# Moving a kernel's stationary blocks by 4 to 124 bytes and its second slot of moving tiles by 32 bytes

## The chip, the cores and the metric

The kernel runs on one core of one Trainium2 chip. The metric is the device time in microseconds of one execution of the whole program; lower is better. The changed kernel computes the same outputs from the same inputs with one launch.

## What is computed

One inference step of a one-layer decoder trunk, for a prompt of 2048 tokens and a group of 64 sample tokens (2112 columns in all), D = 1024 channels, everything in float32:

```python
xn = _rmsnorm(h, norm_mix)
proj = xn @ w_in + b_in                      # 1024 x 9216
q, fz, iv, za, ga, gb, zb, ma, mb = jnp.split(proj, SPLIT_POINTS, axis=-1)
...                                          # recurrence over q, f, v gives o
y_a = (o * jax.nn.silu(za)) @ w_br_a         # 1024 x 1024
u = ga * jax.nn.sigmoid(gb)
...                                          # 31 taps of a depthwise convolution over u give cv
y_b = (cv * jax.nn.silu(zb)) @ w_br_b        # 1024 x 1024
merged = jax.nn.sigmoid(ma) * y_a + jax.nn.sigmoid(mb) * y_b
h = h + merged @ w_o
gate = jax.nn.sigmoid(_rmsnorm(h, norm_ple) @ w_ple_gate)
h = h + gate * (p_l @ w_ple)
```

Nearly all of the work is in the products with w_in, w_br_a and w_br_b (stage 1 and 2 of the kernel) and in those with w_o, w_ple_gate and w_ple (stage 3).

## The kernel before

A float32 product is made of three products in the type fp32r: each operand is split into a high part (a copy rounded to fp32r) and a low part (the rest), and hi*hi, hi*lo and lo*hi are summed in PSUM.

**Weights.** The three big weights are cut into 176 blocks of 128 output columns: 72 of w_in for each half of the tokens, then 16 blocks each of w_br_a and w_br_b. A block is loaded whole into a tile `raw` (128 partitions x 1024 numbers) and split by two instructions in `split_w`: ScalarE (ACT) writes `whi`, VectorE (DVE) writes `wlo`. The pool `wp` turns over three buffers of each; it lies at the right end of SBUF.

```python
    wp = st12.enter_context(tc.tile_pool(name="wp", bufs=3, side="right"))             # L113
    def split_w(b):                                                                    # L323
        b.hi = wp.tile([P, KB, P], F32R, tag="whi", name="whi")
        b.lo = wp.tile([P, KB, P], F32R, tag="wlo", name="wlo")
        nc.scalar.activation(out=b.hi, in_=b.raw, func=AF.Copy)                        # L326
        nc.vector.tensor_tensor(out=b.lo, in0=b.raw, in1=f32(b.hi), op=ALU.subtract)   # L327
```

**Moving tiles.** The activations stand in two slots, X[0] (`x0h`, `x0l`, 512 columns for each of 8 blocks of 128 channels) and X[1] (`x1h`, `x1l`, up to 576 columns), which `x_alloc` (L135) takes from the pool `xres` near the left end of SBUF; they are taken again from the same place for each new half of the tokens and for each stage.

**Units.** A unit is one block of weights times one stretch of 512, 320 or 256 columns of one slot: 24 matmuls (L1357), in which the weights are the stationary operand, loaded anew for every matmul by a LDWEIGHTS, and the slot is the moving one.

```python
        for k in range(KB):                                                            # L1353
            for w, x in ((u.block.hi, xh), (u.block.hi, xl), (u.block.lo, xh)):
                nc.tensor.matmul(ps[:, 0:u.n], lhsT=w[:, k, :], rhs=x[:, k, sl], ...)  # L1357
```

There are 441 units, so 10,584 such matmuls. Between and after them stand small matmuls and transposes of the recurrence (L441 to L594), the convolution's taps on DVE (L686 to L699), and the evacuations of PSUM. The program is ordered by hand: `at_time` gives each piece of side work a unit after which it is issued, and nothing of the order depends on addresses.

**Stage 3** (from L1371) computes the last three products for 17 blocks of tokens with one function `gemm` (L1182, matmuls at L1188). Here the tokens are the stationary operand (`mgi`, `th`, `tl`, `ph`, `pl`) and the weights the moving one (`woh`, `wol`, the slots X[0] and X[1] again, filled with w_ple_gate, and `wph`, `wpl`). Its pools take the room of stage 2 as that is freed. What it loads first is, in the order of SyncE's (SP's) queue: the last store of `mg` to the scratch tensor `mg_dr` (L908), the second `mgi` (L1166, `load_m`), the first `h` (L1175, `load`), then `p`, the second `h`, four loads for w_ple and eight for w_ple_gate (L1382), the norm vector (L1420), and the third `mgi`. The first `h` is needed by the first evacuation of `out_proj` (L1204) and, through a norm on ACT, POOL and DVE (L1281, L1287 to L1289, L1212), by the first transposes of `turn` (L1239).

**Where the tiles lie.** Addresses follow from the sizes of the tiles and the order in which they are taken; a partition holds what is counted here in bytes. In the program as built, all tiles that feed the matmuls of L1357 and L1188 start 96 bytes past a multiple of 128: `x0h` (at 18144), `x0l`, `x1h` (at 50912), `x1l`, the three buffers each of `whi` and `wlo` (from 204768), and in stage 3 `woh`, `wol`, `mgi`, `th`, `tl`, `ph`, `pl`, `wph`, `wpl`. Their slices for k and for columns start at multiples of 128 bytes from there. Among the tiles of the side work, `v`, `st`, `kt` and `kq` start 96 bytes past a multiple of 128 too, `at`, `s_all` and the inputs `xt` 32 bytes past, and `ident` at a multiple of it. `u`, the input of the convolution, starts 96 past a multiple of 128, and tap i reads it from 4*i bytes further on.

Of the kernel before, what the change touches and what calls it, by code (L numbers as in the profile page):

```python
# [9 lines left out]
F32 = mybir.dt.float32  # L10
F32R = mybir.dt.float32r
# [6 lines left out]
P = 128  # L18
KB = 8
# [55 lines left out]
def view(t, off, dims):  # L75
    return bass.AP(t.tensor, t.offset + off, [list(t.ap[0])] + [list(d) for d in dims])


def f32(ap):
    return ap.bitcast(F32)  # L80
# [3 lines left out]
def tile_hybrid_step(  # L84
# [7 lines left out]
    nc = tc.nc  # L92
# [16 lines left out]
    xres = ctx.enter_context(tc.tile_pool(name="xres", bufs=1))  # L109
# [3 lines left out]
    wp = st12.enter_context(tc.tile_pool(name="wp", bufs=3, side="right"))  # L113
# [21 lines left out]
    def x_alloc(slot, cap=None):  # L135
        cap = cap or (512, 576)[slot]
        X[slot] = (xres.tile([P, KB, cap], F32R, tag=f"x{slot}h", name=f"x{slot}h"),
                   xres.tile([P, KB, cap], F32R, tag=f"x{slot}l", name=f"x{slot}l"))
# [74 lines left out]
    x_load(3)  # L213
    every = ("tr", "ab", "kv", "o")
    x_alloc(0)
    x_alloc(1)

    vrow = h1.tile([P, P], F32, tag="sg", name="vrow")
# [102 lines left out]
        nc.sync.dma_start(out=b.raw, in_=b.src.rearrange("(k p) c -> p k c", p=P))  # L321

    def split_w(b):  # L323
        b.hi = wp.tile([P, KB, P], F32R, tag="whi", name="whi")
        b.lo = wp.tile([P, KB, P], F32R, tag="wlo", name="wlo")
        nc.scalar.activation(out=b.hi, in_=b.raw, func=AF.Copy)  # L326
        nc.vector.tensor_tensor(out=b.lo, in0=b.raw, in1=f32(b.hi), op=ALU.subtract)  # L327
        b.raw = None
# [725 lines left out]
    for e in range(2):  # L1054
        x_turn(0, e, every)
    split_w(blocks[0])
    load_raw(blocks[2])
    x_load(6)
# [8 lines left out]
    for i in range(9):  # L1067
        t, b = XOUT0 + XOUT_STEP * i, 8 + i
# [262 lines left out]
    for b in range(1, len(blocks)):  # L1331
        i = 1 if b == 2 else max(uses[b][0] - 3, 0)
        if b >= 3:
            i = max(i, min(uses[b - 3][-1] + 1, uses[b][0] - 1))
        slots.setdefault(i, []).append((1, 0.0, b, lambda b=b: split_w(blocks[b])))
        if b + 2 < len(blocks):
            slots.setdefault(i + RAW_LAG, []).append((4, 0.5, b, lambda b=b: load_raw(blocks[b + 2])))
# [128 lines left out]
```

## Time and profile before

| | us |
|---|---|
| two runs | 2846.43 and 2839.39, median 2842.91 |
| the profiled execution, its own time | 2839.55 |
| span of its profile, first to last instruction | 2837.8 |
| TensorE matmuls (PE) busy | 2791.2 |
| VectorE (DVE) busy | 1886.4 |
| ScalarE (ACT) busy | 930.6 |
| GpSimd (POOL) busy | 544.9 |

The profiled execution takes 1.75 us more than its span, before the first and after the last instruction. A matmul's recorded duration holds its way through the pipeline, so consecutive ones overlap; what one costs in a stream is the distance from its start to the start of the next, which the timeline shows. The two runs lie 7 us apart.

### The profile page before, as it was taken

How to read it: one execution, taken by the hardware profiler on the slowest of the kernel's cores; microseconds unless marked ns; L12 is line 12 of the kernel's file. 1: busy time of each engine (PE TensorE's matmuls, PEld its weight loads, DVE VectorE, ACT ScalarE, POOL GpSimd, SP SyncE). 2: the span in 40 equal slices, each digit the busy share in tenths (PEclk: the TensorE clock that was granted, in tenths of full speed). 3: DMA queues.
4: the chain of work that ended last, by engine and by line, in shares of the span. 5: the costliest groups of instructions: out<-in, count | busy, mean ns of one | idle time of the engine just before them, and what ended most of it. 6: DMA issues, size and time to landing. Idle time of an engine off the chain costs nothing. (4 is left out here: it accounts for less than half of the span.)

```text
span 2837.8 us, 50952 instructions
## 1 busy us (share of the span) xinstructions
PE 2791.2 (98%) x21199; PEld 2383.1 (84%) x21199; DVE 1886.4 (66%) x2994; ACT 930.6 (33%) x2119; POOL 544.9 (19%) x929
## 2 busy tenths in 40 slices
PE   8999999999999999999999999999999999999998
PEld 6888888888888898988888888888789789788887
DVE  6577777777878786666757576677777876433433
ACT  5333333333332432332322322233244443322222
POOL 2000000000000014233240505050536420000000
PEclk9999999999999999999999999999999999999999
DMA  3222222222221422222222222223586879422221
GB/s 122 65 66 82 72 86 90 83 82 64 81 64 59 131 65 74 65 71 66 79 62 65 73 66 69 59 83 103 164 272 208 260 253 299 149 80 78 87 88 39
DMA packets 352799, 292.69 MB, mean 103 GB/s; under 512 B 17514, under 2 KB 301259, under 8 KB 352568
## 3 DMA queue, kind: packets, MB, share of 16 engines
q1 hardware_dynamic: 293856, 218.40, 25.4%
q10 hardware_dynamic: 58440, 70.86, 7.4%
q8 instruction: 166, 2.72, 0.4%
q14 instruction: 65, 0.53, 0.1%
q0 software_dynamic: 272, 0.19, 0.0%
HBM read 201.25 MB, written 88.14 MB: 102 GB/s over the span
## 5 line engine op out<-in xcount | busy, mean ns | idle before, releaser
L696 DVE SCALAR_TENSOR_TENSOR acc<-u,cw,acc 128x512 f32<-128x512 f32 x960 | 726.2, 756 | 24.0
L1357 PE MATMUL mm<-x1h,whi 128*128 128x320 f32 (+2 forms) x2112 | 711.9, 337 | 0.0
L1357 PE MATMUL mm<-x1h,wlo 128*128 128x320 f32 (+2 forms) x2112 | 693.2, 328 | 0.0
L1357 PE MATMUL mm<-x1l,whi 128*128 128x320 f32 (+2 forms) x2112 | 692.7, 328 | 0.0
L1357 PE MATMUL mm<-x0h,whi 128*128 128x512 f32 (+1 forms) x1416 | 564.9, 399 | 1.5 <-ACT x0h L1031 1.1
L1357 PE MATMUL mm<-x0l,whi 128*128 128x512 f32 (+1 forms) x1416 | 551.9, 390 | 2.1 <-DVE x0l L176 1.8
L1357 PE MATMUL mm<-x0h,wlo 128*128 128x512 f32 (+1 forms) x1416 | 551.9, 390 | 0.0
L1357 PEld LDWEIGHTS mm<-x1h,whi 128*128 128x128 f32 x2112 | 401.3, 190 | 33.7 <-issue 4.7
L1357 PEld LDWEIGHTS mm<-x1h,wlo 128*128 128x128 f32 x2112 | 400.6, 190 | 28.7
L1357 PEld LDWEIGHTS mm<-x1l,whi 128*128 128x128 f32 x2112 | 401.5, 190 | 26.4
L327 DVE TENSOR_TENSOR wlo<-raw,whi 128x1024 fp32r<-128x1024 f32 x176 | 218.3, 1241 | 259.6 <-ACT whi L326 253.0
L1357 PEld LDWEIGHTS mm<-x0h,whi 128*128 128x128 f32 x1416 | 266.8, 188 | 59.3 <-ACT sp L780 2.6
L1357 PEld LDWEIGHTS mm<-x0h,wlo 128*128 128x128 f32 x1416 | 266.8, 188 | 56.8 <-DVE wlo L327 0.4
L1357 PEld LDWEIGHTS mm<-x0l,whi 128*128 128x128 f32 x1416 | 267.1, 189 | 53.8 <-DVE x0l L176 2.5
L326 ACT ACTIVATE whi<-raw 128x1024 fp32r<-128x1024 f32 x176 | 186.0, 1057 | 65.7 <-DVE mal L889 23.4
L560 POOL TENSOR_SCALAR ors<-oss 128x4 f32<-128x4 f32 (+1 forms) x40 | 11.6, 289 | 875.5 <-ACT on L558 874.7
L1188 PE MATMUL ps<-woh,mgi 128*128 128x512 f32 x528 | 169.4, 395 | 2.1 <-DMA mgi<-mg_dr 2.1
L419 DVE TENSOR_TENSOR rp<-rp 128x512 f32<-128x512 f32 (+1 forms) x224 | 156.8, 700 | 9.6
L429 DVE TENSOR_TENSOR lvl<-kq,rp 128x512 f32<-128x512 f32 (+2 forms) x224 | 146.8, 655 | 21.2 <-PE d32p L455 19.4
L747 POOL TENSOR_SCALAR nmix<-us,cw 128x64 f32<-128x64 f32 x240 | 156.6, 653 | 0.0
L1188 PEld LDWEIGHTS ps<-woh,mgi 128*128 128x128 f32 x528 | 99.9, 189 | 23.1 <-DMA mgi<-mg_dr 2.4
L780 ACT ACTIVATE sp<-mm,vcol 128x512 f32<-128x512 f32 (+2 forms) x120 | 73.1, 609 | 127.9 <-PE mm L1357 113.0
(254 smaller groups left out, 3345.9 us busy)
## 6 DMA issues: line engine op xcount, KB each, us to landing
raw<-in_w_in_dram SPq DMA_DIRECT2D x144, 512.0 KB, 3.9
mgi<-mg_dr SPq DMA_DIRECT2D x16, 1024.0 KB, 6.0
gate<-am_dr SPq DMA_DIRECT2D x24, 512.0 KB, 5.6
mg_dr<-mg SPq DMA_DIRECT2D x24, 512.0 KB, 3.4
xt<-in_x_prompt_dram SPq DMA_DIRECT2D x16, 512.0 KB, 5.1
g_dr<-gst ACTq DMA_DIRECT2D x32, 256.0 KB, 2.8
cv_dr<-acc ACTq DMA_DIRECT2D x32, 256.0 KB, 2.1
raw<-in_w_br_a_dram SPq DMA_DIRECT2D x16, 512.0 KB, 5.9
```

Of the source, the lines that this page charges most:

```text
L326: nc.scalar.activation(out=b.hi, in_=b.raw, func=AF.Copy)
L327: nc.vector.tensor_tensor(out=b.lo, in0=b.raw, in1=f32(b.hi), op=ALU.subtract)
L419: nc.vector.tensor_tensor(out=io, in0=io, in1=tt, op=ALU.mult)
L429: nc.vector.tensor_tensor(out=o, in0=a, in1=b, op=ALU.mult)
L560: nc.gpsimd.tensor_scalar(out=rs[0:n, 0:m], in0=ss[0:n, 0:m], scalar1=1.0 / P, scalar2=EPS, op0=ALU.mult, op1=ALU.add)
L696: nc.vector.scalar_tensor_tensor(out=self.acc, in0=self.u[:, i:i + G], scalar=w, in1=self.acc, op0=ALU.mult, op1=ALU.add)
L747: nc.gpsimd.tensor_scalar(out=p, in0=self.us[:, :, i:i + 8], scalar1=w, scalar2=None, op0=ALU.mult)
L780: nc.scalar.activation(out=s[:, 0:n], in_=ps[:, 0:n], func=func, bias=bias(kind, j))
L1188: nc.tensor.matmul(ps, lhsT=a[:, k, :], rhs=c[:, k, s], start=(k == 0 and i == 0), stop=(k == kn - 1 and i == len(ops) - 1))
L1357: nc.tensor.matmul(ps[:, 0:u.n], lhsT=w[:, k, :], rhs=x[:, k, sl], start=(k == 0 and w is u.block.hi and x is xh), stop=(k == KB - 1 and w ...
```

## The change

A gap of 8 numbers (32 bytes) is taken between X[0] and X[1], and cleared once by DVE, so that X[1] and all that is taken after it at the left lies 32 bytes further on. The buffers of `whi` and `wlo` become 32 numbers longer, and block i is written to, and read from, an offset of (i mod 32) numbers in its buffer; that is 4*(i mod 32) bytes, so that 32 blocks in turn go through all multiples of 4 from 0 to 124 bytes. So that all of this fits, the room that is kept for descriptors of POOL's DMAs is given as 8192 bytes a partition in place of 16384. The diff:

```diff
     x_alloc(0)
+    gap = xres.tile([P, 8], F32, name="gap")
+    nc.vector.memset(gap, 0.0)
     x_alloc(1)
...
     def split_w(b):
-        b.hi = wp.tile([P, KB, P], F32R, tag="whi", name="whi")
-        b.lo = wp.tile([P, KB, P], F32R, tag="wlo", name="wlo")
+        o = b.i % 32
+        b.hi = view(wp.tile([P, KB * P + 32], F32R, tag="whi", name="whi"), o, [[P, KB], [1, P]])
+        b.lo = view(wp.tile([P, KB * P + 32], F32R, tag="wlo", name="wlo"), o, [[P, KB], [1, P]])
...
-    nc = _bacc.Bacc("TRN2", target_bir_lowering=False, num_devices=1)
+    nc = _bacc.Bacc("TRN2", target_bir_lowering=False, num_devices=1, dynamic_dma_scratch_size=8192)
```

In the program as built, `x0h` and `x0l` still start 96 bytes past a multiple of 128. `x1h` and `x1l` start at a multiple of 128, and so do `woh`, `wol`, `mgi`, `th`, `tl`, `ph`, `pl`, `wph` and `wpl` of stage 3, and `v`, `st`, `kt`, `kq` and `u` of the side work. The weight buffers start 96 past a multiple of 128, 4224 bytes apart, and a block 4*(i mod 32) bytes after that.

No instruction changes its place on any engine. DVE has one more, at its start:

```order
L129 MEMSET mhalf 128x1
L131 MEMSET lead 128x16
L217 MEMSET gap 128x8
L295 MEMSET d32p 128x480
L298 MEMSET lvl_145 128x1152
```

The row of `gap` is new; the others stand as before, with line numbers two higher after it.

The tiles of stage 3 take over other bytes than before, and so some of them wait for something else. This is SP's queue where stage 2 ends, with the semaphores waited for; the eight names DMAHW0 to DMAHW7 are used by SP's DMAs in turn, and DMAHW3 at these rows is the one that the last store of `mg` (the first row) raises when it has landed. Before:

```order
L908 DMA mg_dr<-mg 128x2x320 [waits DMAHW3_49,DVE_49]
L1166 DMA mgi<-mg_dr 128x16x128 [waits DMAHW6_49,DMAHW4_49]
L1175 DMA h<-in_x_prompt_dram 128x1024 [waits DMAHW5_49,DMAHW0_49]
L1180 DMA p<-in_p_prompt_dram 128x256
L1175 DMA h<-in_x_prompt_dram 128x1024 [waits DMAHW7_49]
```

And now:

```order
L911 DMA mg_dr<-mg 128x2x320 [waits DMAHW3_49,DVE_49]
L1169 DMA mgi<-mg_dr 128x16x128 [waits DMAHW4_49,PE_49]
L1178 DMA h<-in_x_prompt_dram 128x1024 [waits DMAHW5_49,DMAHW7_49,DMAHW3_49,DMAHW1_49]
L1183 DMA p<-in_p_prompt_dram 128x256 [waits DMAHW6_49]
L1178 DMA h<-in_x_prompt_dram 128x1024 [waits DMAHW0_49]
```

The first `h` (third row) lies on bytes of an `mg` buffer now, and its load waits until the store in the first row has landed; before, it waited for earlier transfers only. PE's wait in the second row is for a transpose of the recurrence, far back.

## Rows read from the trace of the kernel before

**Rows 1.** The page: busy time by engine, TensorE's granted clock by slice, POOL's DMA queue.

```profile
PE 2791.2 (98%) x21199; PEld 2383.1 (84%) x21199; DVE 1886.4 (66%) x2994; ACT 930.6 (33%) x2119; POOL 544.9 (19%) x929
...
PEclk9999999999999999999999999999999999999999
...
q0 software_dynamic: 272, 0.19, 0.0%
```

**Rows 2.** Groups by line and shape on PE; moving operand first, then stationary.

```profile
line engine op names shapes xcount | busy us, mean ns | idle before us <-releasers
L1357 PE MATMUL mm<-x0h,whi 128*128 128x512 f32 x1400 | 559.0, 399 | 1.1 <-ACT x0h L1031 1.1
...
L1357 PE MATMUL mm<-x1h,whi 128*128 128x512 f32 x704 | 282.6, 401 | 0.0
...
L1357 PE MATMUL mm<-x1h,whi 128*128 128x320 f32 x704 | 223.6, 318 | 0.0
...
L1357 PE MATMUL mm<-x1h,whi 128*128 128x256 f32 x704 | 205.7, 292 | 0.0
...
L1188 PE MATMUL ps<-woh,mgi 128*128 128x512 f32 x528 | 169.4, 395 | 2.1 <-DMA mgi<-mg_dr 2.1
```

**Rows 3.** Timeline of PE, 2376 to 2388 us: 512, then 256 columns (start us, us).

```profile
2375.69 0.39 PE L1357 MATMUL mm<-x0h,wlo 128*128 128x512 f32 x1
...
2384.53 0.39 PE L1357 MATMUL mm<-x0h,wlo 128*128 128x512 f32 x1
...
2384.99 0.28 PE L1357 MATMUL mm<-x1h,wlo 128*128 128x256 f32 x1
...
2387.63 0.31 PE L1357 MATMUL mm<-x1h,whi 128*128 128x320 f32 x1
```

**Rows 4.** Timeline of PE, 1500 to 1502 us: 320 columns.

```profile
1499.80 0.31 PE L1357 MATMUL mm<-x1h,wlo 128*128 128x320 f32 x1
...
1502.00 0.31 PE L1357 MATMUL mm<-x1h,wlo 128*128 128x320 f32 x1
```

**Rows 5.** Timeline of PE after small matmuls of the recurrence, 789 to 792 us.

```profile
789.80 0.40 PE L1357 MATMUL mm<-x0l,whi 128*128 128x512 f32 x1
...
791.89 0.39 PE L1357 MATMUL mm<-x0l,whi 128*128 128x512 f32 x1
```

**Rows 6.** Groups on PEld: the weight loads of L1357.

```profile
L1357 PEld LDWEIGHTS mm<-x1h,whi 128*128 128x128 f32 x2112 | 401.3, 190 | 33.7 <-issue 4.7 <-ACT on L558 0.8
```

**Rows 7.** Groups on PE, 128 columns in plain float32.

```profile
L551 PE MATMUL o<-st,kq 128*128 128x128 f32 x224 | 44.1, 279 | 0.0
...
L551 PE MATMUL o<-s_all,kq 128*128 128x128 f32 x16 | 3.1, 275 | 0.0
```

**Rows 8.** DVE's work on u, by line (duration ns min/median/max); the splits' groups.

```profile
L696 DVE SCALAR_TENSOR_TENSOR acc<-u,cw,acc x960: 740/752/2386, 106.3 to 2050.5; 128x512 f32<-128x512 f32 x192
...
L327 DVE TENSOR_TENSOR wlo<-raw,whi 128x1024 fp32r<-128x1024 f32 x176 | 218.3, 1241 | 259.6 <-ACT whi L326 253.0 <-PE mm L1357 6.1 <-DMA gate<-am_dr 0.5
...
L326 ACT ACTIVATE whi<-raw 128x1024 fp32r<-128x1024 f32 x176 | 186.0, 1057 | 65.7 <-DVE mal L889 23.4 <-DMA am_dr<-mal 12.0 <-DMA raw<-in_w_br_a_dram 10.8
```

**Rows 9.** Timeline of DVE at the program's start; idle time before an instruction in brackets.

```profile
8.06 2.48 DVE L160 SCALAR_TENSOR_TENSOR xt<-xt,xrs,nmix 128x1024 f32<-128x1024 f32 x2 [1.53 <-DMA nmix<-in_norm_mix_dram]
```

**Rows 10.** Timelines of SP, DVE and PE at the seam, and DMA issues there (us to landing).

```profile
2400.82 0.36 SPq L908 DMA_DIRECT2D mg_dr<-mg  x1
...
2401.79 1.66 SPq L1175 DMA_DIRECT2D h<-in_x_prompt_dram  x1
...
2408.83 1.29 DVE L1204 TENSOR_TENSOR h<-ps,h 128x512 f32<-128x512 f32 x2 [8.03 <-DMA h<-in_x_prompt_dram]
2412.12 0.76 DVE L1212 TENSOR_SCALAR hs<-h,rs 128x1024 f32<-128x1024 f32 x1 [2.00 <-POOL rs L1289]
...
2414.13 1.04 PE L1239 MATMUL pt<-ident,hs 128*128 128x128 f32 x8
...
mg_dr<-mg SPq DMA_DIRECT2D x1, 320.0 KB, 2.9
```

## The prediction

> **What bounds the kernel now.** I read the page first: PE is busy for 2791.2 of 2837.8 us, and its granted clock is full, 2.4 GHz, in every slice [rows 1]. No engine and no DMA queue comes near that, so only what lengthens or shortens the stream of matmuls, or makes PE wait, can move the end. Then I read PE's groups by line and shape: L1357 holds nearly all of it, with 1400 triples of 512 columns on slot 0, and on slot 1 704 triples each of 512, 320 and 256 columns [rows 2]; a row's count is of one of three products, so slot 1 has 3 x 3 x 704 = 6336 matmuls. Their mean durations (399, 401, 318, 292 ns) hold the pipeline and are no price. So the timeline comes last, for the distance between starts in an undisturbed stretch. At 512 columns the rows shown are 39 matmuls apart: (2384.53 - 2375.69)/39 = 226.7 ns. At 256 they are 22 apart: 2.64/22 = 120.0 ns [rows 3]. At 320, 15 apart: 2.20/15 = 146.7 ns [rows 4]. At 2.4 GHz and one column a cycle these are 213.3, 106.7 and 133.3 ns plus 13.3 ns each time: a matmul costs its columns and 32 more. All operands of these rows start 96 bytes past a multiple of 128, so the rows do not say whether the 13.3 ns belong to that place or to any. This is what the change touches, and no row answers it directly.
>
> **The change part by part.**
>
> *The gap's memset* is one DVE instruction of 8 columns among the first of the program. DVE idles 1.53 us there until the first loads have landed [rows 9]. It costs nothing; without that cover it would be under 0.1 us.
>
> *The room for descriptors of POOL's DMAs* is halved. POOL issues only its eight small loads at the start, 272 packets and 0.19 MB [rows 1]. I take nothing; if POOL had to wait once for room, about one landing, the 2.9 us that the store in [rows 10] takes, is the most.
>
> *The splits* write and read the weights at offsets of 4 bytes. For DVE there is a row: the taps read `u` at 30 offsets of 4 to 120 bytes, and of 960 the least takes 740 ns and the median 752 [rows 8], so reads at such offsets are no dearer. Writes at them are not shown. If each split took as long again, DVE would gain 176 x 1.24 = 218 us and ACT 176 x 1.06 = 187 us [rows 8], on engines that are busy 1886 and 931 us of 2838 [rows 1]. A block is split three units before its use, some 16 us at 24 x 226.7 ns a unit, which covers 2.3 us. I take nothing.
>
> *Moving operands of slot 1 and of stage 3*, 32 bytes further on. Two groups of L551 have the same weights and a moving tile 96 bytes past a multiple of 128 (`st`, 279 ns) or 32 past it (`s_all`, 275 ns) [rows 7]: hardly a difference, within what waits do to a mean. They are plain float32 and half as wide, so they bound fp32r weakly. Ends: a matmul gets up to 13.3 ns cheaper (the whole extra), or up to 5.5 ns dearer. The latter is the nearest row of the same instruction at another spacing: just after small matmuls the stream runs at (791.89 - 789.80)/9 = 232.2 ns until it settles at 226.7 [rows 5]. I take 0, by [rows 7].
>
> *Stationary operands* at 32 offsets. A load is recorded with 190 ns [rows 6], but follows the one before at the spacing of the matmuls, so a turn of 120 ns is enough for it at 256 columns; at 512 it has 226.7. Whatever a slower load costs is hidden until its turn passes 120 ns, then charged to 256 columns alone, then to 320. Ends: 0, and a load whose recorded 190 ns no longer overlap the one before, in the rival below; by the unsettled spacing of [rows 5], 5.5 ns on all blocks off multiples of 32 bytes, 7/8 x 10,584 x 5.5 ns = 51 us. A gain is the 13.3 ns at most, and only where the moving side allows it. I take 0: moving a reader by 4 bytes left DVE's taps unchanged [rows 8], and the load has time to spare at 512 columns, three in five of the stream's triples.
>
> [...]
>
> *The seam to stage 3* is the only place where waits change. The load of the first `h` now waits for the last store of `mg`. That store is issued at 2400.82 and lands 2.9 us later, at 2403.7; `h` was issued at 2401.79 [rows 10]. So it is 1.9 us late, and with it all that stands behind it on SP: `p`, the second `h`, the loads of w_ple and w_ple_gate, the third `mgi`. `h` itself has some room: `hs` is ready at 2412.12 + 0.76 = 2412.9 and PE comes to its transposes at 2414.13 [rows 10]. The third `mgi` has none, since PE waited 2.1 us for it already [rows 2]. The delays lie on one queue and don't add: between 0 (the loads catch up, with `mgi` out of their way) and 1.9 us. I take 1.9.
>
> *Sum*, against the profiled execution's own 2839.55 us, which lies 3.4 us under the median of the two runs: 2839.55 + 0 + 0 + 0 + 1.9 = 2841.5, so 2842 us. That is no change; about 2% either way is what a measurement of this kernel can tell from none.
>
> **Rivals.**
>
> *Slower: loads become the bound at 256 and 320 columns.* If a load from an offset off 32 bytes loses its overlap with the one before, its turn is the recorded 190 ns [rows 6] in place of 120.0 and 146.7. Of 2112 matmuls at either width 7/8 are hit: 1848 x (70.0 + 43.3) ns = 209 us, so 2839.55 + 209 + 1.9 = 3050 us. For it: those units leave a load the least time [rows 3, 4], and every offset but four is off 32 bytes. [...] It passes 2% (57 us) when a turn reaches 149 ns, as 1848 x (29 + 2) ns = 57 us.
>
> *Faster: the 32 extra columns are the fetch of a line of 128 bytes*, 32 numbers, which a moving row that starts 96 bytes into such a line touches once more (17 for 16 at 512 columns, 11 for 10 at 320, 9 for 8 at 256). Slot 1 and the `woh` of stage 3 then lose it: (6336 + 528) x 13.3 ns = 91 us, so 2750 us. For it: the extra is 13.3 ns at all three widths [rows 3, 4], as one line would be, and none of these operands starts at a multiple of 128. Against it: a fixed cost of changing weights would look the same, and 32 as against 96 bytes made no difference in [rows 7]. It passes 2% from 8.3 ns a matmul.
>
> [...]
>
> *A small loss inside 2%*: the unsettled spacing stays, up to 51 us, 2893 us. It counts with the forecast, as do small gains.
>
> **How the numbers follow.** No change within 2%: 0.72, since no instruction moves and the rows at other offsets [rows 7, 8] show nothing. Slower: 0.19, since 28 of 32 offsets are of a kind that no row shows on PE. Faster: 0.09, since the even 13.3 ns would fit. The forecast's own range is 2818 to 2893: a loss to the end of the unsettled spacing, a gain of about a quarter of the line's 91 us. To the upper side it is stretched to 2915, as the slower case grows from nothing and its smaller sizes lie there; the faster one is left out.
>
> **What would show it.** Starts in undisturbed stretches of L1360 and L1191 at 226.7, 146.7 and 120.0 ns on either slot and for all blocks: right. If they change with the block and come back after 32, the stationary offset counts; if slot 1 differs from slot 0 in every block, the moving one. A rise at 256 and 320 columns alone would be the load. At the seam the first `h` should be issued near 2404 us, and PE's wait for the third `mgi` be up to 1.9 us longer. A rise of the splits' means with ACT or DVE ending PE's waits would show that I was wrong on their cover.

## The result, and the profile after

The changed kernel takes 2865.02 us (median of two runs, 2864.37 to 2865.67) against 2842.91 us: a ratio of 1.0081, with a 95% interval of 1.0056 to 1.0107. That is 22 us slower, inside the 2% and inside the range, but not the "no change" of the forecast. In the later comparisons the kernel before has medians of 2838 to 2840 us (7 to 25 executions each), so the loss is nearer 25 us, which is also what the two profiles differ by.

The page of the changed kernel answers to [rows 1]: PE is busy for 27.8 us more, at the same share of the span (98%) and at the same granted clock, 0.996 in the mean of either trace. DVE, ACT and the weight loads (PEld) are where they were, within 0.1% each.

```profile
PE 2819.0 (98%) x21199; PEld 2382.8 (83%) x21199; DVE 1884.6 (66%) x2995; ACT 930.0 (32%) x2119; POOL 543.9 (19%) x929
...
PEclk9999999999999999999999999999999999999999
```

The groups by line and shape, which answer to [rows 2], say where. The first row of each width is shown, and two of stage 3.

```profile
L1360 PE MATMUL mm<-x0h,whi 128*128 128x512 f32 x1400 | 564.9, 403 | 0.6 <-ACT x0h L1034 0.6
...
L1360 PE MATMUL mm<-x1h,whi 128*128 128x512 f32 x704 | 285.0, 405 | 0.0
...
L1360 PE MATMUL mm<-x1h,whi 128*128 128x320 f32 x704 | 224.0, 318 | 0.0
...
L1360 PE MATMUL mm<-x1h,whi 128*128 128x256 f32 x704 | 204.3, 290 | 0.0
...
L1191 PE MATMUL ps<-woh,mgi 128*128 128x512 f32 x528 | 168.3, 393 | 1.5 <-DMA mgi<-mg_dr 1.5
...
L1191 PE MATMUL ps<-x0h,th 128*128 128x512 f32 x128 | 50.6, 396 | 0.0
...
L1191 PE MATMUL ps<-x1h,th 128*128 128x512 f32 x128 | 49.8, 389 | 0.0
```

The mean at 512 columns is 4 ns up on both slots (399 and 401 before), at 320 it is unchanged, at 256 it is 2 ns down. In stage 3 the products that move `x0h` have 396 ns and those that move `x1h` 389, with the same 128 stationary tiles `th`. In the kernel before the two hardly differ:

```profile
L1188 PE MATMUL ps<-x1h,th 128*128 128x512 f32 x128 | 49.9, 390 | 0.0
...
L1188 PE MATMUL ps<-x0h,th 128*128 128x512 f32 x128 | 49.8, 389 | 0.0
```

The price is in the starts. Three stretches of PE's timeline of the changed kernel follow (start us, us): one of 512 columns on slot 1, a later one on slot 1, and one of 256 columns.

```profile
189.19 0.39 PE L1360 MATMUL mm<-x1h,wlo 128*128 128x512 f32 x1
...
191.91 0.39 PE L1360 MATMUL mm<-x1h,wlo 128*128 128x512 f32 x1
```

```profile
269.07 0.39 PE L1360 MATMUL mm<-x1h,wlo 128*128 128x512 f32 x1
...
271.87 0.40 PE L1360 MATMUL mm<-x1h,wlo 128*128 128x512 f32 x1
```

```profile
1847.38 0.28 PE L1360 MATMUL mm<-x1h,wlo 128*128 128x256 f32 x1
...
1848.80 0.28 PE L1360 MATMUL mm<-x1h,wlo 128*128 128x256 f32 x1
```

Each pair of rows is twelve matmuls apart. The first block (offset 48) runs at 2.72/12 = 226.7 ns, as all did before; the second (offset 72) at 2.80/12 = 233.3; the 256 columns at 1.42/12 = 118.3 against 120.0. In the kernel before, a unit of 24 matmuls wavers for up to some ten of them, as in [rows 5], and then settles: 260 of its 262 undisturbed units of 512 columns do. In the changed kernel 12 of 262 settle. The others repeat a pattern of some three to nine steps, such as 235, 233, 232 ns, to their end, with a mean of 232.1.

Adding up all distances from one start on PE to the next, by the kind of the first matmul, gives 24.6 of the 24.8 us by which the spans differ (2862.6 - 2837.8):

| distances between starts, us | matmuls | before | after | difference |
|---|---|---|---|---|
| slot 0, 512 columns | 3920 | 893.3 | 909.7 | +16.4 |
| slot 1, 512 columns | 1970 | 448.8 | 457.7 | +8.9 |
| slot 1, 320 columns | 2055 | 308.5 | 310.3 | +1.8 |
| slot 1, 256 columns | 2055 | 252.3 | 249.4 | -2.9 |
| stage 3, x0 moving | 399 | 90.4 | 93.1 | +2.7 |
| the rest of stage 3's matmuls | | | | +1.9 |
| distances over 300 ns (waits and halts), and 256 columns on slot 0 | | | | -3.0 |
| side work | | | | -1.2 |

So 25 us of loss lie in the stream at 512 columns, where PE waits for nothing that the profile shows. The busy shares and the waits can't show this: a matmul's recorded time (395 to 405 ns in these groups) overlaps the next one's, which starts 232 ns after it, and a busy share of 98% stays 98%.

### The profile page after: what moved, and what is told of

The parts are those of the page before. It is cut to its first block, busy times and chain, and to the rows that moved or that the text cites. A ratio compares the mean times of both kernels' runs of the same rounds, so it can differ in the third digit from the quotient of the medians.

```text
span 2862.6 us, 50954 instructions
## 1 busy us (share of the span) xinstructions
PE 2819.0 (98%) x21199; PEld 2382.8 (83%) x21199; DVE 1884.6 (66%) x2995; ACT 930.0 (32%) x2119; POOL 543.9 (19%) x929
## 3 DMA queue, kind: packets, MB, share of 16 engines
q8 instruction: 166, 2.72, 0.4%
## 5 line engine op out<-in xcount | busy, mean ns | idle before, releaser
L1360 PE MATMUL mm<-x1h,whi 128*128 128x320 f32 (+2 forms) x2112 | 713.3, 338 | 0.0
L1360 PE MATMUL mm<-x1h,wlo 128*128 128x320 f32 (+2 forms) x2112 | 695.7, 329 | 0.0
L1360 PE MATMUL mm<-x1l,whi 128*128 128x320 f32 (+2 forms) x2112 | 695.6, 329 | 0.0
L1360 PE MATMUL mm<-x0h,whi 128*128 128x512 f32 (+1 forms) x1416 | 571.0, 403 | 1.0 <-ACT x0h L1034 0.6
L1360 PE MATMUL mm<-x0l,whi 128*128 128x512 f32 (+1 forms) x1416 | 558.0, 394 | 1.7 <-DVE x0l L176 1.3
L1360 PE MATMUL mm<-x0h,wlo 128*128 128x512 f32 (+1 forms) x1416 | 558.2, 394 | 0.0
L1360 PEld LDWEIGHTS mm<-x1h,whi 128*128 128x128 f32 x2112 | 400.3, 190 | 36.7 <-issue 4.7
L1360 PEld LDWEIGHTS mm<-x1h,wlo 128*128 128x128 f32 x2112 | 399.2, 189 | 31.1
L1360 PEld LDWEIGHTS mm<-x1l,whi 128*128 128x128 f32 x2112 | 399.8, 189 | 28.9
L330 DVE TENSOR_TENSOR wlo<-raw,whi 128x1024 fp32r<-128x1024 f32 x176 | 218.5, 1242 | 260.1 <-ACT whi L329 259.6
L1360 PEld LDWEIGHTS mm<-x0h,whi 128*128 128x128 f32 x1416 | 267.4, 189 | 64.0 <-ACT sp L783 2.6
L1360 PEld LDWEIGHTS mm<-x0h,wlo 128*128 128x128 f32 x1416 | 267.2, 189 | 62.5 <-DVE wlo L330 0.4
L1360 PEld LDWEIGHTS mm<-x0l,whi 128*128 128x128 f32 x1416 | 267.6, 189 | 58.7 <-DVE x0l L176 2.2
L329 ACT ACTIVATE whi<-raw 128x1024 fp32r<-128x1024 f32 x176 | 186.1, 1058 | 64.1 <-DVE mal L892 31.2
L1191 PE MATMUL ps<-woh,mgi 128*128 128x512 f32 x528 | 168.3, 393 | 1.5 <-DMA mgi<-mg_dr 1.5
L432 DVE TENSOR_TENSOR lvl<-kq,rp 128x512 f32<-128x512 f32 (+2 forms) x224 | 146.7, 655 | 25.3 <-PE d32p L458 23.3
L1191 PEld LDWEIGHTS ps<-woh,mgi 128*128 128x128 f32 x528 | 99.1, 188 | 22.1 <-DMA mgi<-mg_dr 1.8
```

The costliest lines, as they stand in the source:

```text
L432: nc.vector.tensor_tensor(out=o, in0=a, in1=b, op=ALU.mult)
L1191: nc.tensor.matmul(ps, lhsT=a[:, k, :], rhs=c[:, k, s], start=(k == 0 and i == 0), stop=(k == kn - 1 and i == len(ops) - 1))
```

## The experiments

The changed kernel parts the operands in three ways at once: the weight buffers are 4224 bytes long, so they start by turns 224 and 96 bytes past a multiple of 256 (`whi` and `wlo` of one block always 128 apart); the blocks step by 4 bytes; and slot 1 stands 32 bytes further on. All kernels below keep the smaller room for POOL's descriptors. "Distance" is the start of the stationary tile less that of the moving one, modulo 256; in the kernel before it is 0 everywhere in this stream.

**Each part alone.** First the gap, without touching the weights:

```diff
     x_alloc(0)
+    gap = xres.tile([P, 8], F32, name="gap")
+    nc.vector.memset(gap, 0.0)
     x_alloc(1)
```

> Only the 8 numbers between slot 0 and slot 1 (and the smaller room for descriptors). Weight blocks stay where they were, so on slot 0 stationary and moving operand keep their common place. Theory A (the 4-byte steps of the blocks cost): 512 columns stay at 226.7 ns on both slots, time 2843 to 2847 us. Theory B (it is the longer weight buffers, which part the two operands by 128 bytes in some buffers, and not the 4-byte steps): the same, 2843 to 2847. Theory C (the 32 bytes between the operands cost on slot 1): slot 0 stays at 226.7, slot 1 goes to about 232 at 512 columns and about 118 at 256, and the gates of stage 3 on slot 0 to about 233; about 9 - 3 + 3 = 9 us, so 2852 us.

Measured: 2851.4 us, ratio 1.0046 (1.0032 to 1.0061). In its timeline a unit of slot 1 and the next one, of slot 0, stand side by side:

```profile
359.83 0.39 PE L1359 MATMUL mm<-x1h,wlo 128*128 128x512 f32 x1
...
362.63 0.40 PE L1359 MATMUL mm<-x1h,wlo 128*128 128x512 f32 x1
...
365.84 0.39 PE L1359 MATMUL mm<-x0h,wlo 128*128 128x512 f32 x1
...
368.56 0.40 PE L1359 MATMUL mm<-x0h,wlo 128*128 128x512 f32 x1
```

Twelve steps take 2.80 us on slot 1 (233.3 ns) and 2.72 on slot 0 (226.7). Slot 1 has 233.3 in all its 88 units, 256 columns come down to a mean of 116.9. Theory C, which expected 2852 us, holds for the gap; A and B predicted nothing here and so are not enough.

Then the longer buffers, with all blocks at offset 0, at one and the same offset of 4 bytes, and at the 32 offsets:

```diff
-        b.hi = wp.tile([P, KB, P], F32R, tag="whi", name="whi")
+        o = 0        # second kernel: b.i % 32; third: 1
+        b.hi = view(wp.tile([P, KB * P + 32], F32R, tag="whi", name="whi"), o, [[P, KB], [1, P]])
```

(`b.lo` likewise.)

> Only the weight buffers lengthened by 32 numbers, every block at offset 0, no gap: the buffers now lie 4224 bytes apart, and stationary and moving operand differ by 0 or 128 bytes modulo 256, by turns. Theory A (4-byte steps): no change, 512 columns at 226.7 ns, 2843 us. Theory B (the longer buffers): 512 columns near 232 on both slots, about 16 + 9 us more, 2863 us or so. Theory C (the gap): no change, 2843.

> The longer weight buffers and the offset of 4 bytes times (block mod 32), without the gap. Theory A (4-byte steps) and Theory B (longer buffers): 512 columns near 232 ns on both slots, 256 columns near 118 and 320 near 148 on slot 1, 2843 + 20 = 2863 us; stage 3 stays at 226.7. Theory C (the gap makes slot 1's part): slot 0 near 232, slot 1 at 226.7 and 120, 2843 + 16 = 2859.

> The longer weight buffers and one and the same offset of 4 bytes for every block, no gap. Theory A (4-byte steps, each offset with its own pattern): every unit of 512 columns on slot 0 with the pattern that this offset has in the changed kernel, mean 230 to 234 ns, 2860 to 2870 us. Theory B (longer buffers alone): the same time as the kernel with long buffers and offset 0, within 3 us.

Measured: 2862.74 us, ratio 1.0087 (1.0072 to 1.0102), for offset 0; 2861.94, 1.0084 (1.0069 to 1.0099), for the 32 offsets; 2859.38, 1.0075 (1.0058 to 1.0091), for 4 bytes. The timeline with offset 0, fifteen steps of slot 0:

```profile
1388.17 0.40 PE L1358 MATMUL mm<-x0h,wlo 128*128 128x512 f32 x1
...
1391.67 0.40 PE L1358 MATMUL mm<-x0h,wlo 128*128 128x512 f32 x1
```

That is 3.50/15 = 233.3 ns with no offset at all: the lengthening of the buffers, which only made room for the offsets, costs as much as the whole change. B holds: adding the offsets to the long buffers changes the mean distances by next to nothing (231.9 and 232.0 ns on slot 0). (The kernel at 4 bytes lies 3.4 us under the one at offset 0, where B allowed 3; its time alone doesn't part A from B.) Theory A falls as the one cause, but the sweep below shows that the offsets would cost as much without this lengthening. The 233.3 is that of every third block; the other two run at 231.1 to 231.3. This fits three pairs of buffers of which two have `whi` at distance 0 and `wlo` at 128 and one has them the other way round: in every third block the step from the start of (`xh,whi`), during which `whi` is loaded again, is 232.5 ns, and in the others 226.9 to 227.0, as at distance 0. The two losses don't add either (1.0046 and 1.0084 against 1.0081): slot 1's 512 columns, once out of step, pay no more for a second reason (233.3 ns by the gap, 231.9 by the buffers, 232.2 in the changed kernel).

**One cause for both?** Gap and buffers have in common that stationary and moving tile no longer start at equal places. The next three kernels ask whether it is that distance, and modulo what.

The first has longer buffers still, the sweep the same with other offsets:

```diff
-        b.hi = wp.tile([P, KB, P], F32R, tag="whi", name="whi")
+        o = 0        # sweep: b.i % 64
+        b.hi = view(wp.tile([P, KB * P + 64], F32R, tag="whi", name="whi"), o, [[P, KB], [1, P]])
```

The second shifts all by 32 bytes modulo 256, by a pool to the right of `wp`, which moves the weights down by 224 bytes, and a gap of 32 bytes ahead of both slots:

```diff
+    wpad = st12.enter_context(tc.tile_pool(name="wpad", bufs=1, side="right")).tile([P, 56], F32, name="wpad")
+    nc.vector.memset(wpad, 0.0)
     wp = st12.enter_context(tc.tile_pool(name="wp", bufs=3, side="right"))
...
+    gap = xres.tile([P, 8], F32, name="gap")
+    nc.vector.memset(gap, 0.0)
     x_alloc(0)
     x_alloc(1)
```

> The weight buffers lengthened by 64 numbers instead of 32, every block at offset 0, no gap: the buffers lie 4352 bytes apart, and all fp32r operands again start 224 bytes past a multiple of 256, though not at equal places modulo 512 or 4096. Theory P (what counts is the distance from the moving tile to the stationary one, modulo 256): 226.7, 146.7 and 120.0 ns return everywhere, time that of the kernel before within 3 us, so 2835 to 2843. Theory R (it is the length of the buffers or their distance of a power of two): 512 columns stay near 232 ns, 20 to 25 us over the kernel before.

> The buffers of before, but every fp32r operand moved up by 32 bytes, weights too, so that all start at a multiple of 256 and their distances are those of before. Theory P (distance): 226.7, 146.7 and 120.0 ns, time that of the kernel before within 3 us. Theory Q (the place itself: a tile that starts at a multiple of 64 or 128 bytes saves a step of 6.7 ns): 220, 140 and 113.3 ns, some 10,000 x 6.7 = 70 us less. Theory Q' (the place of before was a good one by itself): about 233 ns at 512 columns, some 40 us more.

> Buffers 4352 bytes apart and offsets of 4 bytes times (block mod 64), no gap: one run holds the distances 0, 4, ... 252 bytes from the moving tile to the stationary one, the same for the hi and the lo part. Theory P: only distance 0 (and perhaps 128) gives 226.7 ns at 512 columns, 224 gives 233.3 / 146.7 / 116.7 as the gap gave on slot 1, the others lie between 229 and 237; total 15 to 25 us over the kernel before. If the distance counts modulo 128, offsets 128 to 252 repeat 0 to 124. Theory R (buffers): no dependence on the offset.

Measured: 4352 bytes apart 2838.82 us, ratio 1.0004 (0.9994 to 1.0014); all shifted 2841.51, 1.0009 (1.0000 to 1.0019); the sweep 2863.76, 1.0087 (1.0072 to 1.0102). Twelve steps of slot 0 in the first and eleven in the second:

```profile
1741.24 0.39 PE L1358 MATMUL mm<-x0h,wlo 128*128 128x512 f32 x1
...
1743.96 0.39 PE L1358 MATMUL mm<-x0h,wlo 128*128 128x512 f32 x1
```

```profile
1739.83 0.39 PE L1361 MATMUL mm<-x0h,wlo 128*128 128x512 f32 x1
...
1742.32 0.39 PE L1361 MATMUL mm<-x0l,whi 128*128 128x512 f32 x1
```

226.7 and 2.49/11 = 226.4 ns, within the rows' 10 ns. Buffers longer by 256 bytes cost nothing where buffers longer by 128 cost 25 us, so neither the length by itself matters nor that the buffers lie a power of two apart. Moving everything by 32 bytes costs nothing clear of noise where moving one side costs 13, and it gains nothing either, though every tile then starts at a multiple of 256: R, Q and Q' fall, and P holds at distance 0. In the sweep's timeline, a block at distance 120 and one at 164, twelve steps each:

```profile
417.16 0.39 PE L1358 MATMUL mm<-x0l,whi 128*128 128x512 f32 x1
...
419.88 0.39 PE L1358 MATMUL mm<-x0l,whi 128*128 128x512 f32 x1
```

```profile
560.41 0.40 PE L1358 MATMUL mm<-x0l,whi 128*128 128x512 f32 x1
...
563.27 0.40 PE L1358 MATMUL mm<-x0l,whi 128*128 128x512 f32 x1
```

2.72/12 = 226.7 and 2.86/12 = 238 ns. Distance 0 settles at 226.7 in all its undisturbed units, and so, unforeseen, do 120 and 132; some others do in part of their units; most stand at 230 to 235. Distance 128 does not settle (231.7 to 233.3), so the measure is 256, not 128. Distance 224 gives 233.3, 146.7 and 116.7 ns, what the gap gave on slot 1 (233.3, 146.7 and a mean of 116.9), whose distance is -32. At 256 columns hardly any distance is worse than 0, and the lowest are 113.3 ns, at 64 and 76 and in one of two units at 52. Here `whi` and `wlo` of a block lie at the same distance and the length costs nothing, so the 24 us that this kernel loses are the offsets' own.

The distance does not fix the spacing alone. At distance 156 four of five units of 512 columns settle at 226.7; the fifth repeats six steps (254, 266, 245, 229, 235, 231 ns) to its end, the slowest of all:

```profile
1413.02 0.39 PE L1358 MATMUL mm<-x0l,whi 128*128 128x512 f32 x1
...
1415.94 0.39 PE L1358 MATMUL mm<-x0l,whi 128*128 128x512 f32 x1
```

These twelve steps take 2.92 us, 243.3 ns each. At 16, 100 and 252, too, some units run at 226.7 and some at 230 to 233.3.

**Using it.** Slot 1 has no 512 columns in the second half of the tokens of the stages 1 and 2, so its tiles can be moved there alone:

```diff
+        if slot == 1 and cap == 576:
+            X["n"] = X.get("n", 0) + 1
+            o = 16 if X["n"] % 2 == 0 else 0        # second kernel: 48; third: 19
+            X[slot] = tuple(view(xres.tile([P, KB * 576 + 64], F32R, ...), o, [[576, KB], [1, 576]]) for c in "hl")
+            return
```

> Weights as before; slot 1's tiles start 64 bytes further on, in the second half of the tokens only, where this slot has units of 256 and 320 columns and none of 512. Theory P, with the changed kernel's blocks at distances near 64 bytes (113.3 ns at 256, about 145.6 at 320): 2055 x 6.7 ns + 2055 x 1.1 ns = 16 us less than before, 226.7 ns at 512 columns untouched, about 2822 us. If those blocks were fast for another reason (hi and lo 128 bytes apart): no change, or 116.7 ns and 7 us less.

> As the kernel with 64 bytes, but slot 1's tiles start 192 bytes further on in the second half of the tokens: the distance from the moving tile to the stationary one is then -192, that is 64 modulo 256 (with 64 bytes it was 192). Theory P, by the sweep's rows at distance 64: 113.3 ns at 256 columns, 146.7 at 320, 226.7 at 512; 2055 x 6.7 ns = 14 us less than the kernel before, ratio 0.995. If the sign of the distance does not count: 117.8 ns as with 64 bytes, 4 us less at most. If what the units of 256 columns win is waited for elsewhere: 113.3 ns but less than 7 us.

> The same with 76 bytes, distance 180. Theory P, by the sweep's rows at 180: 143.3 ns at 320 columns, 118.2 at 256, 226.7 at 512; 2055 x (3.4 + 1.8) ns = 11 us less than the kernel before, ratio 0.996. If the sweep's low value at 180 was an accident of its one unit: 146.7 and some 4 us.

Measured: with 64 bytes 2841.1 us, ratio 1.0005 (0.9995 to 1.0014); with 192 bytes 2833.96, 0.9983 (0.9974 to 0.9992); with 76 bytes 2832.87, 0.9979 (0.9970 to 0.9988). Timelines, of 256 columns with 64 bytes (21 steps) and with 192 (18), and of 320 columns with 76 (12):

```profile
1478.64 0.28 PE L1362 MATMUL mm<-x1h,wlo 128*128 128x256 f32 x1
...
1481.12 0.28 PE L1362 MATMUL mm<-x1h,wlo 128*128 128x256 f32 x1
```

```profile
1477.03 0.28 PE L1362 MATMUL mm<-x1l,whi 128*128 128x256 f32 x1
...
1479.07 0.28 PE L1362 MATMUL mm<-x1l,whi 128*128 128x256 f32 x1
```

```profile
1537.10 0.31 PE L1362 MATMUL mm<-x1h,whi 128*128 128x320 f32 x1
...
1538.83 0.31 PE L1362 MATMUL mm<-x1h,whi 128*128 128x320 f32 x1
```

118.1, 113.3 and 144.2 ns. The 16 us expected of 64 bytes failed by a sign of mine: a moving tile 64 bytes further on has distance -64, which is 192, and the sweep has 117.8 ns there, as this kernel does in all 88 units. With 192 bytes the distance is 64, and 65 of 88 units do run at about 113.3 (mean 114.5, highest 117.9). So the sign counts, as the next expectation had it. With 76 bytes 256 columns have 116.7 ns and 320 have 144.5, where the sweep has 118.2 and 143.3 at the same distance of 180: here, too, the distance modulo 256 doesn't say all. The last two kernels are faster than the kernel before, both intervals lying below 1, but by 5 and 6 us, not by 14 and 11. The settled spacing alone would be worth 88 x 24 x (120.0 - 114.5) = 12 us with 192 bytes, and with 76 88 x 24 x (3.3 + 2.2) = 12 us. In the trace of the former the 256-column distances have come down by 9.8 us, and the rest of that execution is up by 4.8, of which 3.8 in distances over 300 ns. As the kernels 4352 bytes apart and all shifted, which change no spacing, differ by 6 us in the same sum, these runs don't tell where the other half stayed.

**How much must be out of step.** With buffers 4352 bytes apart, only `wlo` is moved, by 8 numbers:

```diff
-        o = b.i % 32
-        b.hi = view(wp.tile([P, KB * P + 32], F32R, tag="whi", name="whi"), o, [[P, KB], [1, P]])
-        b.lo = view(wp.tile([P, KB * P + 32], F32R, tag="wlo", name="wlo"), o, [[P, KB], [1, P]])
+        o = 0
+        b.hi = view(wp.tile([P, KB * P + 64], F32R, tag="whi", name="whi"), o, [[P, KB], [1, P]])
+        b.lo = view(wp.tile([P, KB * P + 64], F32R, tag="wlo", name="wlo"), o + 8, [[P, KB], [1, P]])
```

(The removed lines are the changed kernel's; its gap is left out, too.)

> Weight buffers 4352 bytes apart, the hi part at distance 0 from the moving tiles, the lo part 32 bytes further on, no gap. One load in three then has distance 32. Theory P1 (each load pays by its own distance): 512 columns at (2 x 226.7 + 233.3)/3 = 228.9 ns, 9 to 10 us over the kernel before. Theory P2 (a stream settles as a whole, and one operand out of step is enough): 231 to 234 ns, 20 us or more over. Which of the three steps is the long one says with which matmul the lo load meets: the one before its own (moving x lo) or its own (moving x hi).

Measured: 2868.89 us, ratio 1.0104 (1.0090 to 1.0118), the highest of all, though its interval meets those of the other slow kernels, and though two of three loads have distance 0. All 262 units of 512 columns stand at 233.1 to 233.4 ns, so P2 holds. A stretch of its timelines, weight loads first and then matmuls:

```profile
2112.21 0.19 PEld L1358 LDWEIGHTS mm<-x0l,whi 128*128 128x128 f32 x1
2112.44 0.19 PEld L1358 LDWEIGHTS mm<-x0h,wlo 128*128 128x128 f32 x1
2112.68 0.19 PEld L1358 LDWEIGHTS mm<-x0h,whi 128*128 128x128 f32 x1
```

```profile
2112.21 0.40 PE L1358 MATMUL mm<-x0h,whi 128*128 128x512 f32 x1
2112.44 0.40 PE L1358 MATMUL mm<-x0l,whi 128*128 128x512 f32 x1
2112.68 0.39 PE L1358 MATMUL mm<-x0h,wlo 128*128 128x512 f32 x1
```

The load of `wlo` starts with the matmul before its own. Over the whole run the step from the start of that matmul (`x0l,whi`) has a mean of 237.8 ns on slot 0, the one before it 232.2, and that of the lo product itself 228.8; in the kernel before they are 227.6, 227.6 and 228.0. So the matmul that pays most is the one during which the displaced tile is loaded.

The steady spacing of all runs (in each unit the last 12 of its 23 steps, mean over the units without a halt, ns):

| kernel | distance of slot 0; of slot 1 | slot 0, 512 | slot 1, 512 | 320 | 256 | ratio |
|---|---|---|---|---|---|---|
| before | 0; 0 | 226.7 | 226.7 | 146.7 | 120.0 | 1 |
| changed | 0 to 252 | 232.1 | 232.2 | 146.9 | 118.2 | 1.0081 |
| gap only | 0; 224 | 226.7 | 233.3 | 146.7 | 116.9 | 1.0046 |
| long buffers | 0 and 128 | 231.9 | 231.9 | 144.7 | 118.8 | 1.0087 |
| 32 offsets, no gap | 0 to 252 | 232.0 | 232.1 | 146.9 | 118.3 | 1.0084 |
| 4 bytes | 4 and 132 | 233.1 | 233.0 | 146.7 | 118.4 | 1.0075 |
| 4352 apart | 0; 0 | 226.7 | 226.7 | 146.7 | 120.0 | 1.0004 |
| all shifted | 0; 0 | 226.7 | 226.7 | 146.7 | 120.0 | 1.0009 |
| sweep of 64 | 0 to 252 | 232.2 | 232.1 | 146.8 | 118.5 | 1.0087 |
| half 2, 64 bytes | 0; 0, then 192 | 226.7 | 226.7 | 146.7 | 117.8 | 1.0005 |
| half 2, 192 bytes | 0; 0, then 64 | 226.7 | 226.7 | 146.6 | 114.5 | 0.9983 |
| half 2, 76 bytes | 0; 0, then 180 | 226.7 | 226.7 | 144.5 | 116.7 | 0.9979 |
| lo at 32 | 0 and 32 | 233.3 | 233.3 | 146.2 | 118.3 | 1.0104 |

## Why the prediction was wrong, and where it was right

*The step that failed* is the same in two terms: "I take 0, by [rows 7]" for the moving operands and "I take 0" for the stationary ones, by the taps of DVE in [rows 8]. Together they measure 16.4 + 8.9 + 1.8 - 2.9 + 2.7 = 27 us, of the 24.6 that all distances between starts add up to (waits and halts took some back). Both terms asked whether a tile's own place is a dear one; the one other place that was tried for all tiles at once, 32 bytes further on, is not. But in the stream two tiles are in use at once: the load of `wlo` shown above, 0.19 us long, starts at 2112.44, together with the matmul before its own. What the change takes away is their equal start. The rows before could not show that in this stream, since every distance in it was 0. [rows 7] did set two distances side by side (`st` starts 96 bytes past a multiple of 128 like its stationary `kq`, `s_all` 32 past), but in plain float32 at 128 columns, and by recorded durations (279 and 275 ns), which are no spacing: in the stream 399 ns are recorded where the starts are 226.7 apart. The two terms should have been one, with the unsettled spacing as its value, not as its end. Nor do they add: the gap alone costs 13 us, the weights' move alone 24, both together 25.

*The unsettled spacing* was named, at 5.5 ns, as one of the ends and as the third rival, "a small loss inside 2%": up to 51 us. What it described came true: the stream at 512 columns no longer settles at 226.7. Why it would, the prediction did not say. That the 232.2 ns of [rows 5] stand beside 232.1 measured is in part luck, since the changed units do not go on wavering but repeat patterns of their own, from 226.7 to 236.8 ns. The size was off by two: only 512 columns pay, not all 10,584 matmuls, and the units of the kernel before already spend up to some ten of their first matmuls unsettled (mean 227.8, not 226.7, over all). So (5890 matmuls) x (232.2 - 227.8) = 26 us, against the 25.3 of the table's first two rows. The allowance that a multiple of 32 bytes would be free (7/8 of the blocks) was wrong as well: distances 32, 64 and 96 have 233 to 234 ns.

*The lengthening of the buffers* has no term at all. The prediction read it as room for the offsets; alone it costs what the change costs, 25 us.

*The slower rival*, loads as the bound at 256 and 320 columns, fell on its own test: these are the widths that lose next to nothing: 320 columns go from 146.7 to 146.9 ns, and 256 columns gain 1.8.

*The faster rival*, the 32 extra columns as the fetch of a line, falls with the kernel whose tiles all start at a multiple of 256 and which keeps 226.7, 146.7 and 120.0 ns. Rate and extra are in the rows themselves: (226.7 - 146.7)/192 and (146.7 - 120.0)/64 are both 0.417 ns a column, 2.4 columns a ns at a granted clock of 0.996, and 13.3 ns are left at each width. That part of the extra is no fixed price is nevertheless right: 256 columns run at 113.3 ns, half the extra, at distance 64. And the loads have a part in the spacing: moving one load in three by 32 bytes takes this stream from 226.7 to 233.3 ns.

No load is recorded as longer in the changed kernel: PEld's means on the stream are 188 to 190 ns before (L1357) and 189 to 190 after (L1360). The loss is as large at distances of 32 and 128 bytes as at 4: 233.3 ns with `wlo` at 32, 231.9 with one of the two at 128, 233.1 at 4 and 132.

*The splits* cost nothing, as forecast: they start at 4-byte offsets and have means of 1242 and 1058 ns against 1241 and 1057 in [rows 8], and the taps on DVE keep their median of 752 ns.

```profile
L330 DVE TENSOR_TENSOR wlo<-raw,whi x176: 1208/1225/1754, 13.2 to 2394.9; 128x1024 fp32r<-128x1024 f32 x176
```

```profile
L329 ACT ACTIVATE whi<-raw x176: 1040/1057/1084, 12.1 to 2393.8; 128x1024 fp32r<-128x1024 f32 x176
```

(Here min, median and max.) *The memset* takes 0.07 us under the wait for the first loads, and *POOL's room* shows nowhere: the two kernels with equal distances and half the room stand at 1.0004 and 1.0009.

*The seam* went as forecast in its place and cost nothing. SP's timeline there:

```profile
2420.99 4.96 SPq L911 DMA_DIRECT2D mg_dr<-mg  x2
2426.04 0.42 SPq L1169 DMA_DIRECT2D mgi<-mg_dr  x1
2428.50 0.35 SPq L1178 DMA_DIRECT2D h<-in_x_prompt_dram  x1
```

The first `h` is issued 2.0 us after the issue of `mgi` before it ends (2426.46), close to the 1.9. But PE's wait for `mgi` is 1.5 us against 2.1 before (the last number of the L1191 row of `woh`), so the loads catch up and the 1.9 us of the sum were 0.

## What to carry to other kernels

Where a stream loads its weights anew for each matmul (here a load, 0.19 us long, starts with the matmul before its own), ask of any edit that moves a buffer, a length included, whether it changes the distance between the two tiles, not only where each lies. Where equal starts are wanted, as at 512 columns here, lengths that are multiples of 256 bytes keep them (226.7 ns with buffers 4096 and 4352 bytes apart, 231.9 with 4224). Read the loss in the distances between starts: the busy share (98% before and after), the waits (1.5 us for `mgi` after 2.1) and the load rows (188 to 190 ns, then 189 to 190) say nothing of it. Where a trace shows an unsettled stretch beside a settled one (232.2 ns beside 226.7), its difference is a price that the settled state can lose; here it was a better estimate than zero.

## What the hardware showed unforeseen

- Spacing in this stream goes by the distance of the tile being loaded from the tile being read, modulo 256 bytes (226.7 ns with buffers 4352 bytes apart, 231.7 to 233.3 at distance 128) and with its sign (at 256 columns 114.5 ns at 64 and 117.8 at 192, by the two kernels), though not by it alone: at 512 columns 226.7 ns at 0, 120 and 132, elsewhere 228 to 243 with some units at 226.7, and steady means of many units on multiples of 6.7 ns (226.7, 233.3).
- At 512 columns no distance gives less than equal starts do, 226.7 ns; at 256 they are among the worst: 120.0 ns, against 113.3 at distance 64 and 116.7 at 224. At 320 columns they lie between (146.7, with 143 to 153 at others).
- It is a state of the stream, not a sum over matmuls: with one load in three displaced by 32 bytes, the steady mean of the three steps is 233.3 ns, as much as where every load is out of step (233.3 on slot 1 by the gap).
- Open: why the distance matters at all, since no run shows what the load and the read share; why 120 and 132 settle; what, beside the distance, decides between 226.7 and 243.3 ns at 156; and where half of the gain of the last two versions stayed.
